# Two of the five 512-column blocks of w1 and w3 by seven block products in place of eight, in three feed-forward stages of a Trainium2 decoder trunk

## The chip, the cores and the metric

The kernel runs on one core of a Trainium2 chip. The metric is device time in microseconds of one execution, taken as the median over runs of the same program. A core has five engines with a queue of their own each: TensorE (PE; PEld is its weight load), VectorE (DVE), ScalarE (ACT), GpSimd (POOL) and SyncE (SP, which here issues nearly all DMAs). Each queue is worked off in order, and queues wait for each other through semaphores.

## The reference

The reference is a decoder trunk of two layers for 256 tokens of width 1024 in float32. What matters here is the feed-forward stage, which stands twice in each layer:

```
def _swiglu(x, w1, w3, w2):
    return (jax.nn.silu(x @ w1) * (x @ w3)) @ w2
...
    for l in range(DEPTH):
        h = _swiglu(x, ffn_w1[l, 0], ffn_w3[l, 0], ffn_w2[l, 0])
        x = _layernorm(ALPHA * x + 0.5 * h, ln_g[l, 0], ln_b[l, 0])
        h = _mixer(x, l, ...)
        x = _layernorm(ALPHA * x + h, ln_g[l, 1], ln_b[l, 1])
        h = _swiglu(x, ffn_w1[l, 1], ffn_w3[l, 1], ffn_w2[l, 1])
        x = _layernorm(ALPHA * x + 0.5 * h, ln_g[l, 2], ln_b[l, 2])
```

w1 and w3 are 1024 x 2816, w2 is 2816 x 1024. So there are four feed-forward stages and two mixer stages.

## The kernel before

**Numbers in two parts.** Every matrix product is made of three TensorE passes. A float32 value v is split into a rounded part hi and a rest lo = v - hi: ScalarE writes hi (an ACTIVATE Copy to float32r), VectorE writes lo (a TENSOR_TENSOR subtract). `three` then issues hi·x_hi, lo·x_hi and hi·x_lo into one PSUM bank. In a matmul of this kernel the stationary operand is a 128x128 tile of x (128 channels by 128 tokens), and the moving operand is 128 channels by 512 columns of the weight.

**Weights.** `stream` issues one DMA on SP for 128 x 2048 floats (1 MB) into one of four `raw` buffers (`RAW, HL = 4, 8`), and splits it in two pieces of 1024 elements per partition. A piece holds two channel tiles of 512 columns, and takes one of eight `hi` and one of eight `lo` buffers. In the blocks of w1 and w3 the split is made in operations of 512 elements (`sub=512`), elsewhere of 1024. A buffer of `hi` or `lo` comes free when the last matmul that reads it is done, a `raw` buffer when its last split is done.

**A feed-forward stage (`ffn`).** 20 of the 22 column tiles of w1 and w3 are made in five blocks (n = 0 to 4) of 512 columns by `gemm_b2`, the other two by `gemm_a2`; then `gemm_b` multiplies with w2. One block makes a 2 x 2 array of PSUM banks: t = 0, 1 for the two groups of 128 tokens, m = 0, 1 for w1 and w3. Its four MB of weights are loaded in the order (c, m), where c = 0, 1 is the lower and the upper half of the 1024 channels. The pass t = 0 takes them as they come, and the pass t = 1 takes the same pieces again:

```
for t in range(NT):
    order = second if t else (0, 1)
    for c in order:
        for m in range(2):
            if t == 0:
                got[m][2 * c : 2 * c + 2] = stream(srcs[m][:, c * CH : (c + 1) * CH], sub=512, ...)
            for i in range(2 * c, 2 * c + 2):
                rows_b(ps[t][m], t, 2 * i, got[m][i], xh, xl, KT, first=order[0] * KT // 2)
    done(t, ps[t])
```

One `rows_b` is six matmuls, a block 96. After each pass `done` of `front` runs a SiLU on ScalarE out of bank m = 0 (L612 before) and a product with bank m = 1 on VectorE (L613 before). Then `turned` moves the result into the other layout: two copies on GpSimd (`parted`, L193), a transposing DMA on SP (L197), two copies on GpSimd (`joined`, L202), and a split by ScalarE (hhi, L629) and VectorE (hlo, L631). Those results are read only by the product with w2.

**What sets the order.** TensorE's queue is the order of the program text (`manual_schedule`). For the other engines a scheduler places each instruction into its queue, by priorities that rise with every weight chunk (`step`) and by its own model of times; `issue_after` ties a few instructions behind others. Generators that are started with `beside` are continued by `beat`, which counts TensorE's work in units of 1024 moving columns times six matmuls; so the texts `yield 4` and `wait` are distances in TensorE's work.

**The norm ahead of a stage (`Norm`).** The layer norm of the stage before is finished while the next stage begins; `affine` writes the normalised rows in token-last layout (kept in float32 for a while in the tiles `xf` and `nvia`) and splits them into the new x tiles. `front` is 0 for the norm ahead of a mixer and not 0 for the norms ahead of three of the four feed-forward stages; the first stage has none. `tokens` then does four operations of 1024 elements on VectorE (L541 before).

Of the kernel before, what the change touches and what calls it, by code (L numbers as in the profile page):

```python
# [12 lines left out]
F32R = mybir.dt.float32r  # L13
# [4 lines left out]
ALU = mybir.AluOpType  # L18
AX = mybir.AxisListType

P = 128
# [33 lines left out]
def trunk(ctx, tc, x, xT, w13a, w13b, w2, wb, wqk, wu, wg, wgr, wbr, wbrr, wo, gateb, gatebr, sgug, sgub, sguwT, sgubias, lam, diffg,  # L55
# [18 lines left out]
    def name(s):  # L74
        serial[0] += 1
        return f"{s}_{serial[0]}"
# [4 lines left out]
    def side_bank():  # L81
        return psum.tile([P, 512], F32, tag="side", name=name("sbank"))
# [66 lines left out]

        return tc.issue_after(ins) if ins is not None else nullcontext()  # L150

    def stream(src, width=CH, sub=HC, lent=(), after=(None, None), pool=()):

        step()
        raw = raw_pool.tile([P, CH], F32, tag="raw", name=name("raw"))
        for g in gate:
            g[0] -= 1
        while len(gate) > 1 and gate[1][0] < 0:  # L160
            gate.pop(0)
        with behind(gate[0][1] if gate and gate[0][0] < 0 else None):
            loaded[0] = nc.sync.dma_start(raw[:, :width], src).ins
        out = []
        first = sooner.pop() if sooner else latest
        for o in range(0, width, HC):
            eng = G if o // HC in pool else V
            if o // HC in lent:
                hi, lo = ([act.tile([P, 512], F32R, tag="slot", name=name(n)) for _ in range(2)] for n in ("lhi", "llo"))
                at = [(hi[j], lo[j]) for j in range(2)]  # L170
            else:
                hi = hi_pool.tile([P, HC], F32R, tag="hi", name=name("whi"))
                lo = lo_pool.tile([P, HC], F32R, tag="lo", name=name("wlo"))
                at = [(hi[:, p : p + sub], lo[:, p : p + sub]) for p in range(0, HC, sub)]
            for p, (h, w) in zip(range(0, HC, sub), at):
                r = raw[:, o + p : o + p + sub]
                with behind(first[0]):
                    A.activation(h, r, AF.Copy)  # L178
                with behind(after[o // HC] or (first[1] if eng is V else None)):
                    eng.tensor_tensor(out=w, in0=r, in1=h.bitcast(F32), op=ALU.subtract)  # L180
            out.append((hi, lo))
        return out
# [134 lines left out]
    def gemm_b2(srcs, xh, xl, done, norm=None, second=(0, 1), each=None):  # L317
# [9 lines left out]
        for t in range(NT):  # L327
# [14 lines left out]
            with behind(latest[0] if t == 0 else None):  # L342
                done(t, ps[t])

    def gemm_first(srcs, done):

        step()
        ps = [[bank() for _ in range(2)] for _ in range(NT)]
        raw = [[raw_pool.tile([P, CH], F32, tag="raw", name=name("raw")) for _ in range(2)] for _ in range(2)]
        for k0, nk in ((0, 1), (1, 1), (2, 1), (3, 1), (4, 2), (6, 2)):  # L350
            xr = slots("xraw", 2)[0][:, : nk * T]
            nc.sync.dma_start(xr, xT[:, k0 * T : (k0 + nk) * T])
            c, k = k0 // 4, k0 % 4
            if nk == 2 or k % 2 == 0:
                w = [[p.tile([P, HC], F32R, tag=n, name=name("w" + n)) for p, n in ((hi_pool, "hi"), (lo_pool, "lo"))]
                     for _ in range(2)]
            for m in range(2):
                (A if k0 + m == 0 else nc.sync).dma_start(raw[c][m][:, k * 512 : (k + nk) * 512],
                                                          srcs[m][:, k0 * 512 : (k0 + nk) * 512])
            x = x_cat[c][:, k : k + nk]  # L360
            split(x[:, :, :T], x[:, :, T:], xr.rearrange("p (k t) -> p k t", k=nk))
            ws = [[[v[:, (k + j) % 2 * 512 : (k + j) % 2 * 512 + 512] for v in w[m]] for m in range(2)]
                  for j in range(nk)]
            for j in range(nk):
                for m in range(2):
                    split(*ws[j][m], raw[c][m][:, (k + j) * 512 : (k + j + 1) * 512])
            end = k0 + nk == KT
            for ts in ((0,), (1,)) if end else ((0, 1),):
                for j in range(nk):
# [67 lines left out]
    class Norm:  # L437
# [5 lines left out]

        def __init__(self, l, i, scale, eps, after, last=False):
            self.scale, self.eps, self.last, self.done, self.front = scale, eps, last, set(), i
            self.ends, self.xhi, self.xlo = [None] * NT, {}, {}
# [97 lines left out]
        def sent(self):  # L544
# [15 lines left out]
            self.affine(1, 0, self.via[1], self.via[1], (1, 1, 2), two[1])  # L560
            yield 1.7
            self.affine(1, 1, self.via[2], self.via[2], (2, 2), two[2])

        def affine(self, t, h, src, xf, pieces, two=None):
            self.done.add((t, h))
            k = 0
            with soon():
                for n in pieces:
# [30 lines left out]
    def ffn(l, f, i, norm, last=False):  # L599
# [445 lines left out]
```

## Time and profile before

| | |
|---|---|
| runs | median 1209.9 us, 1209.68 to 1210.15 (3 runs) |
| profiled execution | span 1208.3 us from its first to its last instruction; the page gives no device time of this execution beside it |
| PE busy | 1202.6 us, 5891 matmul records |
| DVE busy | 903.2 us (75%) |
| ACT busy | 719.9 us (60%) |
| POOL busy | 332.9 us (28%) |
| granted TensorE clock | 1.000 over the span |
| DMA | 263.58 MB, mean 218 GB/s |

A matmul's record is longer than the distance to the next, since matmuls are pipelined. So PE's busy time tells only that something was in the array; its pace is read from the distance of the block ends. In the first of the three stages that the change touches, layer 0's second feed-forward stage, the blocks lie as follows (by the SiLU operations at their ends): n = 1 from 441.9 us, n = 2 from 463.7, n = 3 from 485.5, n = 4 from 507.2 to 529.0.

### The profile page before, as it was taken

Reading aid. Unit: us, or ns where it says so; the run is one execution under the profiler, and the core shown is the slowest. Engines: PE = TensorE matmul, PEld = TensorE weight load, DVE = VectorE, ACT = ScalarE, POOL = GpSimd, SP = SyncE. Lnnn points to the kernel's source line nnn. Section 1 sums busy time; section 2 is a strip of 40 time slices with the busy share of each in tenths; the row PEclk is TensorE's granted clock in tenths of the full one; section 3 lists DMA queues with packets and bytes.
Section 4 is the critical chain, followed back from the end, with each engine's and each line's share of the span. In section 5 each row is a group of like instructions: output and inputs, shape, how many; then the busy total and the mean of one; then the engine's idle time right before and its main releaser. Section 6 shows DMA issues by size and latency. Waiting matters only on the chain.

```text
span 1208.3 us, 16816 instructions
## 1 busy us (share of the span) xinstructions
PE 1202.6 (100%) x5891; PEld 1013.3 (84%) x5891; DVE 903.2 (75%) x1544; ACT 719.9 (60%) x1388; POOL 332.9 (28%) x442
## 2 busy tenths in 40 slices
PE   9999999999999999999999999999999999999998
PEld 8888888888888888888888888888888888888887
DVE  6686669897689886766686756688966989776763
ACT  6465547668855665554555554576788556564740
POOL 1433101256421234330053330004464012423300
PEclk9999999999999999999999999999999999999999
DMA  9967646768765666767476766476676764877540
GB/s 347 303 219 238 253 174 203 259 200 231 240 213 180 200 231 208 249 201 261 149 245 198 259 187 261 148 273 238 211 205 199 251 192 153 274 231 239 186 181 35
DMA packets 124006, 263.58 MB, mean 218 GB/s; under 512 B 88417, under 2 KB 89489, under 8 KB 97809
## 3 DMA queue, kind: packets, MB, share of 16 engines
q1 hardware_dynamic: 119664, 248.80, 62.0%
q0 software_dynamic: 3824, 13.18, 3.4%
q8 instruction: 46, 0.75, 0.3%
q10 hardware_dynamic: 432, 0.52, 0.1%
q14 instruction: 40, 0.32, 0.1%
HBM read 236.52 MB, written 1.05 MB: 197 GB/s over the span
## 4 chain that ended last, share of the span: by engine, by line
PE 99%; DMA 0%; DVE 0%; ACT 0%; issue 0%; ACTq 0%
PE bank L256 72%; PE bank L268 15%; PE bank L275 8%; PE bank L374 2%; PE sbank L704 1%; PE sbank L760 1%; PE sbank L878 1%; DMA xraw<-in_xT 0%; PE sbank L758 0%; PE sbank L533 0%; PE sbank L512 0%; DVE xtok L520 0%; ACT whi L220 0%; DVE st L471 0%; DVE xtok L467 0%; ACT x L220 0%
## 5 line engine op out<-in xcount | busy, mean ns | idle before, releaser
L180 DVE TENSOR_TENSOR wlo<-raw,whi 128x512 fp32r<-128x512 f32 (+1 forms) x566 | 524.6, 962 | 114.8 <-ACT whi L178 80.0
L178 ACT ACTIVATE whi<-raw 128x512 fp32r<-128x512 f32 (+1 forms) x570 | 433.3, 799 | 246.6 <-PE bank L256 183.0
L256 PE MATMUL bank<-whi,x 128*128 128x512 f32 x1480 | 460.7, 390 | 0.0
L256 PEld LDWEIGHTS bank<-whi,x 128*128 128x128 f32 x1480 | 277.9, 188 | 57.7
L256 PE MATMUL bank<-wlo,x 128*128 128x512 f32 x740 | 288.0, 389 | 0.0
L256 PEld LDWEIGHTS bank<-wlo,x 128*128 128x128 f32 x740 | 139.0, 188 | 28.2
L268 PE MATMUL bank<-x,whi 128*128 128x512 f32 x640 | 153.3, 391 | 0.0
L256 PE MATMUL bank<-whi,hhi 128*128 128x512 f32 (+1 forms) x374 | 141.2, 378 | 0.0
L256 PE MATMUL bank<-wlo,hhi 128*128 128x512 f32 (+1 forms) x374 | 141.0, 377 | 0.0
L256 PE MATMUL bank<-whi,hlo 128*128 128x512 f32 (+1 forms) x374 | 140.9, 377 | 0.0
L193 POOL COPY planes<-planes 128x512 uint16<-128x512 uint16 x80 | 87.1, 1116 | 193.9 <-DVE planes L613 193.9
L268 PEld LDWEIGHTS bank<-x,whi 128*128 128x128 f32 x640 | 118.2, 188 | 23.8
L202 POOL COPY planes<-planes 128x512 uint16<-128x512 uint16 x80 | 70.9, 931 | 95.8 <-DMA planes<-planes 95.5
L613 DVE TENSOR_TENSOR planes<-planes,bank 128x512 f32<-128x512 f32 x40 | 27.4, 684 | 83.8 <-issue 69.3
L612 ACT ACTIVATE planes<-bank 128x512 f32<-128x512 f32 x40 | 23.9, 598 | 102.6 <-PE bank L256 101.5
L275 PEld LDWEIGHTS bank<-x,wlo 128*128 128x128 f32 x640 | 81.4, 191 | 2.9
L275 PE MATMUL bank<-x,wlo 128*128 128x256 f32 x640 | 82.6, 283 | 0.0
L256 PEld LDWEIGHTS bank<-whi,hlo 128*128 128x128 f32 x374 | 70.4, 188 | 13.0
L256 PEld LDWEIGHTS bank<-whi,hhi 128*128 128x128 f32 x374 | 70.4, 188 | 12.8
L256 PEld LDWEIGHTS bank<-wlo,hhi 128*128 128x128 f32 x374 | 70.4, 188 | 12.6
L575 POOL COPY nvia<-ntwo 128x256 uint16<-128x256 uint16 x20 | 10.4, 565 | 198.1 <-DMA ntwo<-nvia 179.9
L680 POOL TENSOR_TENSOR swap<-swap,sin_t 128x512 f32<-128x512 f32 x16 | 27.1, 1695 | 100.0 <-DMA swap<-z 78.0
(209 smaller groups left out, 1392.0 us busy)
## 6 DMA issues: line engine op xcount, KB each, us to landing
raw<-in_w13b SPq DMA_DIRECT2D x76, 1024.0 KB, 5.8
raw<-in_w SPq DMA_DIRECT2D x40, 1024.0 KB, 6.2
raw<-in_wb SPq DMA_DIRECT2D x16, 1024.0 KB, 5.1
raw<-in_wqk SPq DMA_DIRECT2D x16, 1024.0 KB, 6.3
raw<-in_w13a SPq DMA_DIRECT2D x8, 1024.0 KB, 5.1
raw<-in_wgr SPq DMA_DIRECT2D x8, 1024.0 KB, 5.3
raw<-in_wg SPq DMA_DIRECT2D x8, 1024.0 KB, 5.0
raw<-in_wu SPq DMA_DIRECT2D x8, 1024.0 KB, 6.4
```

The source lines that it names most:

```text
L178: A.activation(h, r, AF.Copy)
L180: eng.tensor_tensor(out=w, in0=r, in1=h.bitcast(F32), op=ALU.subtract)
L193: G.tensor_copy(out=planes(out)[:, w], in_=numbers(src)[:, w])
L202: eng.tensor_copy(out=numbers(out)[:, w], in_=planes(src)[:, w])
L256: PE.matmul(ps, xx, w, start=start and n == 0, stop=stop and n == 2)
L268: PE.matmul(b[-1], hi[:, k * P : (k + 1) * P], xc(k), start=k == 0, stop=False)
L275: PE.matmul(b[n][:, :T], lo[:, k * P : (k + 1) * P], xc(k)[:, :T], start=False, stop=k == KT - 1)
L374: PE.matmul(ps[t][m], x[:, j, o + t * P : o + (t + 1) * P], y, start=k0 + j == 0 and o == 0 and y is hi, stop=k0 + j == KT - 1 and y is lo)
L612: silu[0] = A.activation(s, ps[0], AF.Silu).ins
L613: added[0] = V.tensor_tensor(out=s, in0=s, in1=ps[1], op=ALU.mult).ins
L680: turned_by[0] = G.tensor_tensor(out=s3, in0=s3, in1=s, op=ALU.mult).ins
L704: PE.matmul(banks[m][:, j * nk : (j + 1) * nk], rows(qT, m, j, t * P, P), rows(kT, m, j, 0, nk), start=True, stop=True)
```

## The change

In the stages whose norm has `front` not 0 (layer 0 second, layer 1 first and second feed-forward stage), the blocks n = 2 and n = 4 are made by a new function, `gemm_seven`. It takes the 2 x 2 block form (x in token groups by channel halves, the weight in channel halves by w1, w3) and makes seven products of four channel tiles each, with 12 matmuls each, in place of eight. The sums on the weight side are made for each block by `differ` on VectorE, in place in the raw buffers. The sums on the x side are made once per stage by `Norm.seven`. Three side banks of PSUM are used; results are copied out by `kept` (ScalarE) and added on VectorE. The waits of the transposing steps of block n = 1 are one unit shorter in these stages.

```diff
+    def differ(out, a, b):
+        for o in range(0, CH, HC):
+            V.tensor_tensor(out=out[:, o : o + HC], in0=a[:, o : o + HC], in1=b[:, o : o + HC], op=ALU.subtract)
+
+    def gemm_seven(srcs, sums, done):
+        x11, x12, x22 = ((lambda k, o, h=h, t=t: x_cat[h][:, k, o + t * P : o + (t + 1) * P])
+                         for t, h in ((0, 0), (0, 1), (1, 1)))
+        s1, s2, s3, s4 = (lambda k, o, v=v: v[bool(o)][:, k * P : (k + 1) * P] for v in sums)
+        bx, by, bz = (side_bank() for _ in range(3))
+
+        def product(ps, x, w, first):
+            for k in range(KT // 2):
+                hi, lo = (v[:, k % 2 * 512 : k % 2 * 512 + 512] for v in w[k // 2])
+                for n, (y, o) in enumerate(((hi, 0), (lo, 0), (hi, T))):
+                    PE.matmul(ps, x(k, o), y, start=first and k == n == 0, stop=k == KT // 2 - 1 and n == 2,
+                              skip_group_check=True)
+                beat(0.25)
+
+        def kept(ps):
+            v = s512("part")
+            A.activation(v, ps, AF.Copy)
+            return v
+
+        (w11, w21), (w12, w22) = ((s[:, :CH], s[:, CH:]) for s in srcs)
+        w11 = fetch(w11)
+        product(bx, x11, pieces(w11), True)
+        w12 = fetch(w12)
+        differ(w11, w12, w11)
+        product(bz, s1, pieces(w11), True)
+        a, z = kept(bx), kept(bz)
+        w22 = fetch(w22)
+        differ(w11, w22, w11)
+        product(bx, s2, pieces(w11), False)
+        b = kept(bx)
+        product(bz, s4, pieces(w22), False)
+        w21 = fetch(w21)
+        differ(w12, w22, w12)
+        product(bx, s3, pieces(w12), False)
+        c = kept(bx)
+        product(by, x12, pieces(w21), True)
+        differ(w11, w21, w11)
+        V.tensor_tensor(out=a, in0=by, in1=a, op=ALU.add)
+        V.tensor_tensor(out=b, in0=bz, in1=b, op=ALU.add)
+        done(0, (a, b))
+        V.tensor_tensor(out=c, in0=c, in1=z, op=ALU.add)
+        product(bx, x22, pieces(w11), False)
+        done(1, (bx, c))
...
+            if self.front:
+                yield 4
+                yield from self.seven()
...
+        def seven(self):
+            x11, x12, x21, x22 = (self.rows[v] for v in ((0, 0), (0, 1), (1, 0), (1, 1)))
+            self.sums = [slots("sum", 4, F32R) for _ in range(4)]
+            for v, (out, a, b, op) in zip((0, 2, 1, 3), ((x22, x21, x22, ALU.add), (x21, x11, x21, ALU.subtract),
+                                                         (x11, x22, x11, ALU.subtract), (x12, x12, x11, ALU.subtract))):
+                V.tensor_tensor(out=out, in0=a, in1=b, op=op)
+                split(*self.sums[v], out)
+                yield 1
...
+            elif n in (2, 4) and norm:
+                gemm_seven(srcs, norm.sums, front(n, (10.3, 10.3)))
             else:
-                gemm_b2(srcs, xh, xl, front(n, (13.3, 10.3)), norm=norm if n == 0 else None)
+                early = norm is not None and n == 1
+                gemm_b2(srcs, xh, xl, front(n, (13.3 - early, 10.3 - early)), norm=norm if n == 0 else None)
```

`fetch` is the loading part of `stream`, taken out of it. `pieces` splits one raw buffer into two hi and two lo buffers with operations of 1024 elements. In the changed file these lines have other numbers: `split` is L225 (ScalarE) and L227 (VectorE), `differ` L363, the matmul of `product` L381, `kept` L387, the three additions L408, L409 and L411, the SiLU L696, the product behind it L697, hlo L715.

In the built program of the changed kernel VectorE's queue has, at the end of such a block (block n = 2 of the stage above; out<-in, rows that follow each other):

```
L227 TensorTensor wlo<-raw,whi 128x1024           (w21, first half)
L227 TensorTensor wlo<-raw,whi 128x1024           (w21, second half)
L363 TensorTensor raw<-raw,raw 128x1024 x2        (difference for the seventh product)
L408 TensorTensor part<-sbank,part 128x512        (a = by + a; waits for the sixth product's last matmul)
L409 TensorTensor part<-sbank,part 128x512        (b = bz + b)
L411 TensorTensor part<-part,part 128x512         (c = c + z)
L697 TensorTensor planes<-planes,part 128x512     (SiLU(a) times b)
L227 TensorTensor wlo<-raw,whi 128x1024           (seventh product, first half)
L227 TensorTensor wlo<-raw,whi 128x1024           (seventh product, second half)
```

More of the change, by code (lines that the diff above doesn't have):

```diff
@@ L150, in behind, with fetch @@
         return tc.issue_after(ins) if ins is not None else nullcontext()
-    def stream(src, width=CH, sub=HC, lent=(), after=(None, None), pool=()):
+    def fetch(src, width=CH):
         step()
@@ L163, in stream @@
             loaded[0] = nc.sync.dma_start(raw[:, :width], src).ins
+        return raw
+    def stream(src, width=CH, sub=HC, lent=(), after=(None, None), pool=()):
+        raw = fetch(src, width)
         out = []
@@ L343, in gemm_b2, with pieces @@
                 done(t, ps[t])
+    def pieces(raw):
+        out = []
+        for o in range(0, CH, HC):
+            hi = hi_pool.tile([P, HC], F32R, tag="hi", name=name("whi"))
+            lo = lo_pool.tile([P, HC], F32R, tag="lo", name=name("wlo"))
+            split(hi, lo, raw[:, o : o + HC])
+            out.append((hi, lo))
+        return out
+    def differ(out, a, b):
+        for o in range(0, CH, HC):
+            V.tensor_tensor(out=out[:, o : o + HC], in0=a[:, o : o + HC], in1=b[:, o : o + HC], op=ALU.subtract)
[39 more added lines that the diff above has]
+        done(1, (bx, c))
     def gemm_first(srcs, done):
@@ L445, in __init__ @@
             self.scale, self.eps, self.last, self.done, self.front = scale, eps, last, set(), i
-            self.ends, self.xhi, self.xlo = [None] * NT, {}, {}
+            self.ends, self.xhi, self.xlo, self.rows = [None] * NT, {}, {}, {}
             self.gT, self.bT = (v[:, l, i] for v in (ln_g, ln_b))
@@ L562, in sent @@
             self.affine(1, 1, self.via[2], self.via[2], (2, 2), two[2])
+            if self.front:
+                yield 4
+                yield from self.seven()
         def affine(self, t, h, src, xf, pieces, two=None):
             self.done.add((t, h))
+            self.rows[t, h] = xf
             k = 0
```

## Prediction

> **What bounds the kernel now.** I read the page first: the busy times, the slices and the chain of work that ended last.
>
> ```profile
> span 1208.3 us, 16816 instructions
> PE 1202.6 (100%) x5891; PEld 1013.3 (84%) x5891; DVE 903.2 (75%) x1544; ACT 719.9 (60%) x1388; POOL 332.9 (28%) x442
> PE 99%; DMA 0%; DVE 0%; ACT 0%; issue 0%; ACTq 0%
> ```
>
> TensorE is the bound: 99% of the chain, with nothing to name between its matmuls. What a matmul is worth is read from the distance of block ends, in ScalarE's timeline (start, duration, what was waited for):
>
> ```profile
> 452.82 0.60 ACT L612 ACTIVATE planes<-bank 128x512 f32<-128x512 f32 x1 [7.01 <-PE bank L256]
> 463.70 0.60 ACT L612 ACTIVATE planes<-bank 128x512 f32<-128x512 f32 x1 [0.16 <-PE bank L256]
> 474.58 0.60 ACT L612 ACTIVATE planes<-bank 128x512 f32<-128x512 f32 x1 [6.55 <-PE bank L256]
> L256 PE MATMUL bank<-whi,x 128*128 128x512 f32 x1480 | 460.7, 390 | 0.0
> ```
>
> Each pass of 48 matmuls takes 10.88 us, a block 21.76, a matmul 10.88 / 48 = 0.2267 us; its record is 0.390 long, so its end lies 0.16 after the next could start. Then I asked for the four blocks n = 1 to 4 of this stage (columns: length, then busy time and count by engine):
>
> ```profile
> 441.90:463.70 21.80, 21.80 (x98) 18.05 (x97) 17.69 (x26) 10.24 (x19) 11.07 (x8) 1.00 0.65 196
> 463.70:485.50 21.80, 21.80 (x98) 18.03 (x97) 14.69 (x25) 11.35 (x23) 6.59 (x8) 1.00 0.68 239
> 485.50:507.20 21.70, 21.70 (x97) 18.00 (x96) 15.07 (x23) 11.27 (x22) 6.75 (x8) 1.00 0.66 217
> 507.20:529.00 21.80, 21.80 (x97) 18.03 (x97) 14.40 (x19) 10.88 (x18) 6.72 (x8) 1.00 0.70 203
> ```
>
> VectorE (third pair) has 7 us to spare in a block of 21.8, and only 4 in n = 1, where the norm is still being finished. That slack is what the change spends.
>
> **Part 1, what is removed.** Each of six blocks (two in each of three stages) issues 7 x 12 = 84 matmuls of the same shape in place of 96. 12 x 0.2267 = 2.72 us a block, 16.3 us in all, at full value, since nothing else is on the chain. A block would take 19.04 us.
>
> **Part 2, what VectorE gets.** Prices, from its timeline (the first two rows give pitches by their starts):
>
> ```profile
> 448.01 1.21 DVE L541 TENSOR_TENSOR xtok<-xtok,bc 128x1024 f32<-128x1024 f32 x1
> 449.15 0.68 DVE L180 TENSOR_TENSOR wlo<-raw,whi 128x512 fp32r<-128x512 f32 x1
> 449.75 1.21 DVE L541 TENSOR_TENSOR xtok<-xtok,bc 128x1024 f32<-128x1024 f32 x1
> 450.89 1.88 DVE L180 TENSOR_TENSOR wlo<-raw,whi 128x512 fp32r<-128x512 f32 x3
> 469.90 0.74 DVE L631 TENSOR_TENSOR hlo<-planes,hhi 128x256 fp32r<-128x256 f32 x2
> 530.87 1.23 DVE L180 TENSOR_TENSOR wlo<-raw,whi 128x1024 fp32r<-128x1024 f32 x1 [0.92 <-ACT whi L178]
> ```
>
> So 1024 wide: pitch 1.14, duration 1.23. 512 wide: 0.60 and 0.68. hlo: 0.37. A block had 16 lo subtractions of 512 (9.6 us), two products behind the SiLU (1.2) and four hlo (1.5), 12.3 bare. It gets 14 lo subtractions and 8 differences of 1024 (25.1), three additions (1.8), and the same products and hlo: 29.6 bare, against 19.04 of TensorE. Some of it can be done ahead. How much, the built order says: behind the seven wide operations that serve the first two products stands the SiLU product of the block ahead, which waits for that block's last matmul. Everything later is made while TensorE works.
>
> I walk that queue for one block, time 0 being the start of the first product. The SiLU can start at 0.16 and takes 0.60; VectorE's product is issued at 0.8, the next operation at 1.4. Up to the additions follow two differences and two lo for the third product, two lo for the fourth, two for the fifth (its differences were made ahead), two for the sixth, two differences for the seventh, and four hlo: 12 x 1.14 + 4 x 0.37 = 15.2. Since each difference must land before ScalarE can round it, a little is lost: I allow 0.8. VectorE reaches the additions at 17.4. TensorE ends its sixth product at 6 x 2.72 + 0.16 = 16.5. So without any disturbance VectorE is just behind.
>
> GpSimd disturbs it:
>
> ```profile
> 499.87 1.49 POOL L193 COPY planes<-planes 128x512 uint16<-128x512 uint16 x2 [3.72 <-DVE planes L613]
> 489.02 2.72 DVE L180 TENSOR_TENSOR wlo<-raw,whi 128x512 fp32r<-128x512 f32 x3
> 489.24 1.96 POOL L193 COPY planes<-planes 128x512 uint16<-128x512 uint16 x2 [9.63 <-DVE planes L613]
> 532.01 0.68 DVE L613 TENSOR_TENSOR planes<-planes,bank 128x512 f32<-128x512 f32 x1
> 532.61 3.27 DVE L180 TENSOR_TENSOR wlo<-raw,whi 128x1024 fp32r<-128x1024 f32 x2
> ```
>
> A pair of copies takes 1.49, 0.75 each. Three lo that take 1.88 alone take 2.72 beside a pair; two wide ones take 3.27 for 1.14 + 1.23 = 2.37. A pair thus costs VectorE 0.84 to 0.90, if it meets a full queue. Up to three of a block's four pairs fall ahead of the additions: 0 to 2.5 us. [...]
>
> **Part 3, the wait that is added.** The three additions and the first SiLU product stand ahead of the seventh product's two lo subtractions, and the first addition waits for the sixth product's last matmul. Behind it queue exactly the operands of the next 12 matmuls. From the moment when VectorE is free and that matmul has ended: 3 x 0.60 + 0.60 + 1.23 = 3.63 until the first lo lands. TensorE can run one matmul (hi) meanwhile. Were VectorE early, the stall would be 0.16 + 3.63 - 0.2267, with semaphores some 3.7 us: more than the 2.72 saved. ScalarE's SiLU of a (0.60) runs beside the second and third addition. With VectorE at the additions at 17.4 the lo lands at 21.0 where TensorE wanted it at 16.6: a loss of 4.5. The parting copies of the first SiLU product start with these two lo, as in the last row above: 0.45 on the first, 0.45 on the second, of which the second is mostly covered by the half product (1.36). So 5.0 undisturbed before. With one and a half pairs of copies ahead of the additions I take 1.6 more: **6.6 us a block** (bounds 3.7, VectorE early, and 7.5, all pairs meet it).
>
> **Part 4, the rest.** Norm.seven adds four sums and four splits of 512 a stage, 8 x 0.60 = 4.8 on VectorE in block n = 1, where 4.1 were free and the work ahead now has four wide differences more (4.6). Part of it shifts into the lead: I take 1 us a stage (bounds 0 and 3). ScalarE: 14 roundings of 1024, three copies and two SiLU of 512 (0.60 each) and four hhi a block, from
>
> ```profile
> L178 ACT ACTIVATE whi<-raw 128x1024 fp32r<-128x1024 f32 x5 | 5.3, 1064 | 4.1 <-PE bank L256 4.1
> L629 ACT ACTIVATE hhi<-planes 128x256 fp32r<-128x256 f32 x12 | 4.6, 407 | 0.0
> raw<-in_w13b SPq DMA_DIRECT2D x76, 1024.0 KB, 5.8
> ```
>
> 14.9 + 3.0 + 1.6 = 19.5, less than VectorE's share and inside the longer block: nothing. A copy out of PSUM must end before the bank is written again; one product (2.72) lies between and covers 0.6; without it 0.6 each. Loads: their number and sizes stay, but the raw buffers are held longer. The last one, w11, is free when the seventh lo is made, about 23; 5.8 later it holds the last quarter of the next block, wanted three quarters of a pass later, at 25 + 8.2 = 33: hidden with 4 us to spare; any lateness beyond that would be paid one for one. What the copies and transposes give is read by w2's product alone, behind the whole stage: nothing.
>
> **Part 5, the clock.** TensorE was idle for long only at the very end (its last timeline row, and two windows behind it, where the third number from the end is the granted clock):
>
> ```profile
> 1202.97 1.56 PE L512 MATMUL sbank<-bc,minus 128*128 128x256 f32 x4 [0.66 <-ACT minus L510]
> 1204.50:1207.30 2.80, 0.02 (x1) 0.00 (x0) 0.75 (x1) 0.00 (x0) 0.00 (x0) 1.00 0.51 187
> 1207.40:1208.30 0.90, 0.00 (x0) 0.00 (x0) 0.00 (x0) 0.00 (x0) 0.00 (x0) 0.50 0.00 0
> ```
>
> The last matmul ended at 1204.5, and 2.8 us later the clock was halved. The new stalls leave TensorE idle for 3.7 us and more, so I expect this inside the kernel. How long it lasts no row shows; if as long as the idle time that brought it, 2.8 us at half pace lose 1.4. I take 1.5 for four of the six: 6 us (bounds 0 and 6 x 3). [...]
>
> **Sum**, against the profiled execution's span: 1208.3 - 16.3 + 6 x 6.6 + 3 x 1 + 6 = 1240.6. The median of the runs lies 1.6 above that span, so 1242.
>
> **Rivals.** *Stalls without the clock* (28%): as above with a clock at 1.00; 1242 - 6 = 1236. For: the drop was seen once only, and the idle stretches are broken by one matmul. *VectorE is early* (10%): copies miss its full stretches and its lead is larger; only the floor is lost, 1209.9 - 16.3 + 6 x 3.7 = 1216. Against: 29.6 bare us a block. *Heavy* (10%): all pairs meet it, n = 1 pays 3, every stall costs 3 us of clock: 1209.9 - 16.3 + 45 + 9 + 18 = 1266. *Faster* (4%): the seventh product's lo are not late, because the stage behind the addition is shorter than rows say. It decides at 2.72: if wait, additions and lo took TensorE less than that, the change would win; were it 1.5, 1209.9 - 16.3 + 9 = 1203. For: VectorE's other halves, such as operations of 256, are short. Against: each of the five operations has its row, and none may overtake in a queue that is worked off in order. *No change* (3%) needs the same chain at 2.3 to 3.1. That the change removes fewer matmuls than it says can be left out: the built program has 5671 in place of 5743, 72 less.
>
> **How the numbers follow.** Forecast with the clock 45%, without it 28, early 10, heavy 10, faster 4, same 3. The range must leave out at most 2 in 10: it cuts the faster and same cases, half of the early and most of the heavy one: 1217 to 1262. Slower by over 0.2% (2.4 us, about what a measurement of this kernel tells from no change): 93%.
>
> **What would show it.** In the profile after: six gaps on PE of 3.7 us or more, each in L381 behind its first matmul on the seventh product, ended by VectorE's lo (L227), behind L408 to L411 and L697; blocks n = 2 and n = 4 of 25 to 27 us, n = 3 near 22; DVE near full in them; PEclk below 1.00 in slices of the three stages. I am wrong if these blocks take under 21.8, if PE waits there for DMA, or if the gaps sit at the first products, which would put it down to VectorE's lead and not to the order.

## The result and the profile after

| | before | after |
|---|---|---|
| median | 1209.9 us | 1257.9 us (1257.13 to 1259.01, 4 runs) |
| ratio | | 1.0398, 95% interval 1.0383 to 1.0413 |
| profiled execution, span | 1208.3 us | 1255.4 us |
| mean granted TensorE clock | 1.000 | 0.985 |

The changed kernel is 48 us slower: the forecast of 1242 had the direction right and was 16 us short, inside its range. The page of the changed kernel first (the span; busy times by engine; the granted clock in 40 slices):

```profile
span 1255.4 us, 16779 instructions
PE 1212.1 (97%) x5819; PEld 1009.8 (80%) x5819; DVE 1032.8 (82%) x1622; ACT 767.1 (61%) x1412; POOL 390.8 (31%) x442
PEclk9999999999999999989999999999999999979999
```

VectorE is busy for 130 us more, and TensorE is no longer busy throughout. The view of waits on TensorE names what it waits for (engine, tile and line; us in total, times, longest one):

```profile
PE sbank L381 <- DVE wlo L227: 29.2, 12, 4.0
PE bank L261 <- DVE silu L283: 2.6, 3, 1.1
```

The kernel before has no such wait in these stages. Twelve waits for VectorE's lo are two for each of the six blocks: the forecast had one each. The windows of the six blocks, from their first matmul to the next block's (start:end, length, busy time and count of PE, PEld, DVE, ACT, POOL, then granted clock, DMA share, GB/s):

```profile
467.09:495.64 28.55, 21.56 (x86) 16.66 (x84) 28.55 (x30) 20.15 (x30) 9.70 (x8) 0.94 0.48 141
517.78:545.11 27.33, 22.43 (x86) 17.28 (x85) 27.33 (x29) 18.85 (x25) 8.98 (x6) 0.89 0.54 162
662.59:689.48 26.89, 21.77 (x85) 16.75 (x84) 26.89 (x28) 18.94 (x29) 9.17 (x8) 0.94 0.53 152
711.92:740.59 28.67, 23.11 (x85) 17.91 (x84) 27.35 (x28) 18.94 (x25) 9.46 (x7) 0.88 0.51 142
1094.06:1125.75 31.69, 25.03 (x85) 19.38 (x84) 29.07 (x31) 20.18 (x30) 10.44 (x8) 0.79 0.48 139
1147.70:1174.70 27.00, 22.32 (x86) 16.45 (x84) 27.00 (x28) 18.47 (x25) 11.71 (x7) 0.94 0.51 148
```

The blocks take 26.9 to 31.7 us in place of 21.8 before, and VectorE is busy for all of it in four of them. At 0.2267 us for each matmul a block would take 19.04. What the starts of the matmuls show beyond that is about 6.7 us of stall a block (40.1 in all: 2.1 at the third product and 4.5 at the seventh, the remainder at a few single matmuls) and about 15.5 us in all of matmuls at half clock. VectorE's timeline shows the first of these blocks (start, duration, form; rows without a bracket followed at once on the one before):

```profile
467.16 1.21 DVE L227 TENSOR_TENSOR wlo<-raw,whi 128x1024 fp32r<-128x1024 f32 x1
468.29 1.21 DVE L363 TENSOR_TENSOR raw<-raw,raw 128x1024 f32<-128x1024 f32 x1
469.43 1.21 DVE L227 TENSOR_TENSOR wlo<-raw,whi 128x1024 fp32r<-128x1024 f32 x1
470.56 0.67 DVE L697 TENSOR_TENSOR planes<-planes,bank 128x512 f32<-128x512 f32 x1
471.16 2.76 DVE L363 TENSOR_TENSOR raw<-raw,raw 128x1024 f32<-128x1024 f32 x2
...
484.68 2.35 DVE L363 TENSOR_TENSOR raw<-raw,raw 128x1024 f32<-128x1024 f32 x2
486.95 0.68 DVE L408 TENSOR_TENSOR part<-sbank,part 128x512 f32<-128x512 f32 x1
487.56 0.68 DVE L409 TENSOR_TENSOR part<-sbank,part 128x512 f32<-128x512 f32 x1
488.15 0.68 DVE L411 TENSOR_TENSOR part<-part,part 128x512 f32<-128x512 f32 x1
488.75 1.18 DVE L697 TENSOR_TENSOR planes<-planes,part 128x512 f32<-128x512 f32 x1
489.86 3.27 DVE L227 TENSOR_TENSOR wlo<-raw,whi 128x1024 fp32r<-128x1024 f32 x2
```

The SiLU product of the block ahead (L697 at 470.56) stands 3.47 us behind the block's start, where the prediction had 0.8: VectorE was not waiting for it but still at the second product's operands. ScalarE's SiLU had long been done:

```profile
464.57 0.60 ACT L696 ACTIVATE planes<-bank 128x512 f32<-128x512 f32 x1 [0.91 <-PE bank L261]
```

It reads only the bank of w1, which is complete 12 matmuls before the block ends at 467.09. So the block ends that were read from the SiLU operations of the kernel before lie some 2.5 us early (by TensorE's timeline its n = 2 starts at 466.22 and not at 463.70); their distances, and with them the price of a matmul, are not touched by that.

Since VectorE is behind, the differences for the third product come late, TensorE waits there, and again at the seventh, where the additions stand before the lo:

```profile
474.06 0.50 PE L381 MATMUL sbank<-whi,sum 128*128 128x512 f32 x1 [1.37 <-ACT part L387]
475.86 0.50 PE L381 MATMUL sbank<-wlo,sum 128*128 128x512 f32 x1 [1.30 <-DVE wlo L227]
...
487.10 0.50 PE L381 MATMUL sbank<-whi,x 128*128 128x512 f32 x1 [0.29 <-ACT whi L225]
491.63 0.79 PE L381 MATMUL sbank<-wlo,x 128*128 128x512 f32 x1 [4.03 <-DVE wlo L227]
```

### The profile page after: what moved, and what is told of

It is laid out like the page before. It is cut to its first block, busy times and chain, and to the rows that moved or that the text cites. A ratio compares the mean times of both kernels' runs of the same rounds, so it can differ in the third digit from the quotient of the medians.

```text
span 1255.4 us, 16779 instructions
## 1 busy us (share of the span) xinstructions
PE 1212.1 (97%) x5819; PEld 1009.8 (80%) x5819; DVE 1032.8 (82%) x1622; ACT 767.1 (61%) x1412; POOL 390.8 (31%) x442
## 5 line engine op out<-in xcount | busy, mean ns | idle before, releaser
L185 DVE TENSOR_TENSOR wlo<-raw,whi 128x1024 fp32r<-128x1024 f32 (+1 forms) x470 | 462.9, 1021 | 82.4 <-ACT whi L183 62.5
L183 ACT ACTIVATE whi<-raw 128x512 fp32r<-128x512 f32 (+1 forms) x474 | 375.8, 833 | 191.9 <-PE bank L261 126.8
L261 PE MATMUL bank<-whi,x 128*128 128x512 f32 x1096 | 343.2, 390 | 0.0
L261 PEld LDWEIGHTS bank<-whi,x 128*128 128x128 f32 x1096 | 206.0, 188 | 42.2
L261 PE MATMUL bank<-wlo,x 128*128 128x512 f32 x548 | 214.1, 391 | 1.2 <-DVE wlo L185 1.1
L198 POOL COPY planes<-planes 128x512 uint16<-128x512 uint16 x80 | 122.9, 1563 | 132.0 <-DVE planes L697 132.0
L207 POOL COPY planes<-planes 128x512 uint16<-128x512 uint16 x80 | 92.5, 1201 | 155.4 <-DMA planes<-planes 155.4
L225 ACT ACTIVATE whi<-raw 128x1024 fp32r<-128x1024 f32 (+1 forms) x100 | 97.1, 988 | 54.4 <-DVE raw L363 46.6
L227 DVE TENSOR_TENSOR wlo<-raw,whi 128x1024 fp32r<-128x1024 f32 (+1 forms) x100 | 120.5, 1232 | 4.8 <-ACT whi L225 4.6
L261 PEld LDWEIGHTS bank<-wlo,x 128*128 128x128 f32 x548 | 103.0, 188 | 25.4 <-DVE wlo L185 4.4
L381 PE MATMUL sbank<-whi,sum 128*128 128x512 f32 x192 | 65.2, 412 | 3.3 <-ACT part L387 3.2
```

The source lines that it names most:

```text
L198: G.tensor_copy(out=planes(out)[:, w], in_=numbers(src)[:, w])
L207: eng.tensor_copy(out=numbers(out)[:, w], in_=planes(src)[:, w])
L225: a = A.activation(hi, src, AF.Copy).ins
L227: return a, eng.tensor_tensor(out=lo, in0=src, in1=hi.bitcast(F32), op=ALU.subtract).ins
L261: PE.matmul(ps, xx, w, start=start and n == 0, stop=stop and n == 2)
L381: PE.matmul(ps, x(k, o), y, start=first and k == n == 0, stop=k == KT // 2 - 1 and n == 2, skip_group_check=True)
```

## The experiments

The theories at the start: **A, the order** (the additions and the SiLU product ahead of the seventh product's lo); **B, the amount** of VectorE's work, whatever its order; and **C, the half clock**. In the short diffs, lines are shortened to what changes.

**1. The order alone.** The seventh product's lo are issued ahead of the additions and the SiLU product.

```diff
+        seventh = pieces(w11)
+        with behind(halved[0]):        # halved: the last lo of those pieces
             V.tensor_tensor(out=a, in0=by, in1=a, op=ALU.add)
...
-        product(bx, x22, pieces(w11), False)
+        product(bx, x22, seventh, False)
```

> The seventh product's two lo subtractions are put ahead of the three additions and the first SiLU product in VectorE's queue (the additions are issued behind the second lo). Nothing else changes. Theory A (order: the stall of 3.5 to 4.5 us on the seventh product is made by the additions' wait for the sixth product): the lo land 3.3 us earlier, the idle stretches fall under 1.5 us, the granted clock goes back to about 1.00, and the time falls by 6 x 3.3 + 14 = 34 us, to about 1224. Theory B (amount: VectorE is simply full, and the order decides only where TensorE waits): what is saved on the seventh product is paid in the next block; 1245 to 1255, with new gaps in blocks n = 3.

Measured: 1241.75 us (1240.78 to 1242.83), ratio to before 1.0264, 1.0247 to 1.0281. The order is worth 16.2 us, 2.7 a block, and 32 us of loss stay. The distance of the first two matmuls of the seventh product, 3.5 to 4.5 us in the changed kernel, falls to 1.3 at most; the stall at the third product stays; and a new wait stands at the start of n = 3 (waits on TensorE):

```profile
PE sbank L383 <- DVE wlo L227: 11.6, 12, 1.4
PE bank L261 <- DVE wlo L185: 8.3, 6, 2.5
```

It lies between the two forecasts, 1224 by A and 1245 to 1255 by B, and has the new gaps in n = 3 that B expected: both are at work.

**2. The amount alone.** `differ` does nothing, so the products are made with the plain weights. The scheduler then places the seventh product's lo ahead of the additions by itself.

```diff
     def differ(out, a, b):
-        for o in range(0, CH, HC):
-            V.tensor_tensor(out=out[:, o : o + HC], ..., op=ALU.subtract)
+        pass
```

> The weight differences are left out (the products take the raw weights, so the output differs): 8 operations of 1024 elements less per block on VectorE. In the built order the scheduler then also puts the seventh product's lo ahead of the additions. Both theories: with amount and order relieved nothing is left to wait for; the 72 matmuls come out in full, 1209.9 - 16.3 = 1194, up to 1198 with the sums of the norm. Above 1200 would mean a third cost (banks, loads).

Measured: 1213.72 us, ratio 1.0032, 1.0019 to 1.0045. All six blocks take exactly 19.04 us, without a stall. But the time is 16 to 20 us above what was expected, so there is a third cost. The waits on TensorE and TensorE's own timeline put it at the start of w2, after block n = 4; ScalarE's and SP's queues show why:

```profile
PE bank L261 <- DVE silu L283: 11.0, 3, 3.7
```
```profile
541.33 0.79 PE L261 MATMUL bank<-whi,hhi 128*128 128x512 f32 x1 [3.68 <-DVE silu L283]
```
```profile
539.49 1.06 ACT L183 ACTIVATE whi<-raw 128x1024 fp32r<-128x1024 f32 x1 [6.50 <-DMA raw<-in_w]
540.45 0.37 ACT L281 ACTIVATE r<-bank 128x256 f32<-128x256 f32 x1
```
```profile
532.64 1.23 SPq L202 DMA_TRANSPOSE planes<-planes  x1
533.97 0.53 SPq L161 DMA_DIRECT2D raw<-in_w  x1
```

VectorE's product of the last two column tiles (L283) waits for L281, which stands on ScalarE behind a rounding that waits for a piece of w2 for 6.5 us; that piece's load is issued at 533.97, behind a transposing DMA of block n = 4. In the kernel before the two outputs of a block come 11 us apart; by seven both come at its end, and so do their transposes.

**3. That third cost.** As experiment 2, with the transposing DMAs of n = 4 one unit of TensorE's work later, behind w2's first four loads on SP.

```diff
-                gemm_seven(srcs, norm.sums, front(n, (10.3, 10.3)))
+                gemm_seven(srcs, norm.sums, front(n, (11.3, 11.3) if n == 4 else (10.3, 10.3)))
```

> As e2_no_differ (no differences on the weight side, the seventh product's lo ahead of the additions), and for n = 4 the transposing DMAs of a pass are issued later (11.3 in place of 10.3), so that on SP all four loads of w2's first pieces stand ahead of them. Theory: e2's rest against the bare 16.3 us of gain, 20 us, lies at the start of w2, where the fourth load stands behind a transposing DMA and ScalarE's queue behind that load; three waits of 3.9 and the half clock of 5.3 behind them go, at most 17 us: 1197 to 1203. Rival: the wait is for the last block's own chain (SiLU, copies, transposes all at the block's end), whichever queue it stands in: 1212 to 1215.

Measured: 1196.78 us (1196.18 to 1197.5), ratio 0.9893, 0.9880 to 0.9907. The theory holds. SP now has

```profile
521.50 5.35 SPq L161 DMA_DIRECT2D raw<-in_w  x4
533.29 1.23 SPq L202 DMA_TRANSPOSE planes<-planes  x1
```

and no wait at w2 is left. This also prices the half clock where TensorE is the bound: experiment 2 had waits of 11.0 us and lost about 5.3 us in matmuls at half clock behind them, 16.3 together, and its profiled span is 16.5 us longer (1211.0 against 1194.5). And nearly the whole saving of the 72 matmuls comes out: in full it would give 1209.9 - 16.3 = 1193.6, and 3.2 of it are lost elsewhere.

**4. The same edit with the differences back**, the whole computation: experiment 1 with the later transposes.

> The whole computation: as e1_lo_first, with the same later transposing DMAs for n = 4. Theory: the wait of 1.5 us at the start of w2 goes in three stages, 1241.75 - 4.5 = 1237. Rival: VectorE's amount of work is the bound in these stages and the wait only moves: 1241 to 1242.

Measured: 1241.14 us, ratio 1.0258, 1.0244 to 1.0272. Nothing is gained against experiment 1. The rival has the right number, but the wait didn't move: it stayed at the start of w2, 3.9 us in three waits against 4.1 before the edit, though the four loads now stand ahead of the transposes on SP. With the differences VectorE itself is late there; its product L283 follows six lo subtractions without a pause:

```profile
544.35 8.55 DVE L185 TENSOR_TENSOR wlo<-raw,whi 128x1024 fp32r<-128x1024 f32 x6
552.82 0.41 DVE L283 TENSOR_TENSOR silu<-bank,r 128x256 f32<-128x256 f32 x1
```

Against experiment 3 the only difference in the work is `differ`: 48 operations of 1.14 us, 54.7 us on VectorE, cost 44.4 us of time. (The additions are tied behind the lo here; in experiment 3 the scheduler put them later by itself, among the lo of the next block. Experiment 12 tries a later place with the differences and gains nothing.)

**5. The order without the differences.** As experiment 2, with the additions and the SiLU product held ahead of the seventh product's lo as in the changed kernel.

```diff
-            split(hi, lo, raw[:, o : o + HC])
+            split(hi, lo, raw[:, o : o + HC], after=(None, hold))
...
-        product(bx, x22, pieces(w11), False)
+        product(bx, x22, pieces(w11, added[0]), False)   # added: the SiLU product
```

> As the kernel without differences, but the seventh product's lo are issued behind the first SiLU product, so that the order of the changed kernel is restored while VectorE has 9 us less per block. Theory A: the floor of the stall stays, one addition, the SiLU, the product and one lo after the sixth product, about 3.3 us a block: 1194 + 6 x 3.3 = 1214, and some us of lowered clock, 1214 to 1225. Theory B: VectorE has time to spare, the order costs next to nothing: 1194 to 1200.

Measured: 1244.81 us, ratio 1.0291, 1.0275 to 1.0306. Against experiment 2 the order costs 31.1 us, 5.2 a block, and not the 3.3 of the additions and lo alone, because VectorE's queue also waits for ScalarE's SiLU, which the scheduler put behind the next block's roundings, and these wait for a load (ScalarE, then VectorE):

```profile
483.44 2.19 ACT L183 ACTIVATE whi<-raw 128x512 fp32r<-128x512 f32 x4 [0.83 <-DMA raw<-in_w13b]
485.53 0.61 ACT L695 ACTIVATE planes<-part 128x512 f32<-128x512 f32 x1
```
```profile
486.17 0.69 DVE L696 TENSOR_TENSOR planes<-planes,part 128x512 f32<-128x512 f32 x1 [2.47 <-ACT planes L695]
```

With experiments 1 and 2 and the changed kernel this is a two by two table:

| | additions first | lo first |
|---|---|---|
| with differences | 1257.9 | 1241.75 |
| without | 1244.8 | 1213.7 |

The last cell holds some 17 us of w2's start, which experiment 3 takes away and which experiment 5 doesn't have (no wait for L283 in its list). With experiment 3's 1196.8 in that cell the order costs 48 us without the differences and 16 with them, and the differences cost 13 us with the additions first and 45 with the lo first. So the costs of order and amount can't be added: they hide each other, since both make VectorE late for the same matmuls.

**6. The clock alone.** The changed kernel with 14 matmuls more, into a spare bank, behind the first matmul of the seventh product, so that the array isn't idle there.

```diff
+                    for _ in range(fill if k == n == 0 else 0):
+                        PE.matmul(spare, x(0, 0), x_cat[0][:, 0], start=True, stop=True, ...)
...
-        product(bx, x22, pieces(w11), False)
+        product(bx, x22, pieces(w11), False, fill=14)
```

> Behind the first matmul of each seventh product TensorE runs 14 matmuls into a bank that nobody reads (3.2 us, less than each of the stalls of 3.5 to 4.5 us there). The work and all waits stay. If the lowered clock of the changed kernel (39 us of the span at 0.50) comes from these idle stretches and costs what the slower matmuls add up to (16 us): the clock stays at 1.00 and the time falls to about 1243. If the clock in the records costs nothing, or follows something else: 1257 to 1260.

Measured: 1261.48 us (1258.81 to 1263.63), ratio 1.0423, 1.0407 to 1.044. Within the span the time at half clock falls from 37.5 to 20.5 us (from 11 pieces of 3.41 us to 6), matmuls lose about 9 us to it in place of about 16, and nothing comes back. The time went to the next places that need VectorE: the three blocks n = 3 take 3.9 us more than in the changed kernel, and the waits on TensorE show the start of w2 (2.6 us there in the changed kernel):

```profile
PE sbank L381 <- DVE wlo L227: 12.1, 11, 1.4
PE bank L261 <- DVE silu L283: 8.0, 3, 2.9
```

So theory C gets no support in this kernel: where VectorE is late, half of the half clock could go without any gain in time. The other half stayed, so this is shown for half of it only. (The 14 matmuls, 3.3 us, fit into the gap and delay nothing by themselves except where it was shorter.)

**7. The fixed cost.** All blocks by `gemm_b2` as before, with the sums on the x side kept.

```diff
-            elif n in (2, 4) and norm:
+            elif False:
```

> All five blocks of a stage by gemm_b2 as before; the four sums and their splits on the x side (Norm.seven) stay, and so do the shorter waits of n = 1. It measures the change's fixed cost by itself. The prediction's Part 4 has 1 us a stage (0 to 3): 1213, at most 1219. The trace after shows n = 0 and n = 1 together 0.5 to 1.3 us longer in each stage, 2.5 in all: 1212.5. Rival: the lengthening of n = 1 is VectorE's lead for the first block by seven (the work ahead for n = 2) and not the sums; then 1210 to 1211.

Measured: 1212.09 us against 1209.64, ratio 1.0020, 1.0011 to 1.0029: 2.45 us, 0.8 a stage.

**8. A difference on GpSimd.** As experiment 4, with the fifth product's difference (w22 - w12) by GpSimd.

```diff
-        differ(w12, w22, w12)
+        differ(w12, w22, w12, G)
```

> As e7_lo_first_late, with one of the four differences of each block (w12 - w22, the operand of the fifth product) made by GpSimd in place of VectorE. VectorE is given 2.28 us less a block. If GpSimd needs 0.75 per 512 elements as in its copies, it works 3 us a block longer and holds VectorE up by 0.43 for each 0.75, 1.7 us: a net gain of 0.6 a block, 3.4 us below e7. Rival: it is slower than that, the fifth product waits for it and VectorE is held up for longer than the difference took: 3 us or more above e7.

Measured: 1258.2 us, ratio 1.0399, 1.0383 to 1.0415: 17 us slower than experiment 4. One pair of operations after another, from the timelines of VectorE and GpSimd, and the longest entry of the waits on TensorE:

```profile
466.34 3.37 POOL L365 TENSOR_TENSOR raw<-raw,raw 128x1024 f32<-128x1024 f32 x1
467.37 3.43 DVE L365 TENSOR_TENSOR raw<-raw,raw 128x1024 f32<-128x1024 f32 x1
469.67 3.36 POOL L365 TENSOR_TENSOR raw<-raw,raw 128x1024 f32<-128x1024 f32 x1
470.73 3.39 DVE L227 TENSOR_TENSOR wlo<-raw,whi 128x1024 fp32r<-128x1024 f32 x1
```
```profile
PE sbank L383 <- DVE wlo L227: 22.6, 12, 2.4
```

Beside VectorE, GpSimd's subtraction takes 3.36 us, and VectorE's operation beside it takes as long, in place of 1.2. In the whole kernel VectorE is busy for 1040.9 us, against 1030.2 in experiment 4, with 12 operations less. The rival is right that VectorE is held up for longer than the difference took. But the fifth product never waits for GpSimd's result: by the starts of the matmuls the stalls lie in the second and third product of each block, whose lo VectorE makes at that time.

**9. Half of the differences.** As experiment 4 without the first two differences of each block.

> As e7_lo_first_late, without the first two of the four differences of each block (the operands of the second and the third product are then the plain weights, the output is another). VectorE is given 4.56 us less a block, 25.0 bare in place of 29.6; without any difference it was 20.5. Theory L, VectorE's amount is paid in proportion: half of the 44.4 us between e7 (1241.1) and e6 (1196.8): 1219. Rival T, a threshold: a block by seven and the plain block before or behind it give VectorE 19.0 + 21.8 = 40.8 us of TensorE's work for 25.0 + 14.7 = 39.7 us of its own, so it just keeps up, the stalls at the third product go with its two differences, and what is left is paid little: 1205 or less. Rival S, the stalls belong to the seventh product's own two differences and to the order there: 1230 or more.

Measured: 1224.07 us (1220.73 to 1225.61), ratio 1.0114, 1.0097 to 1.0131; undecided, since another wait came in. No third product waits any more, but the first matmul of every seventh product waits for the copy of the fifth product's bank, which ScalarE had behind next-block roundings and a rounding that waits for VectorE (waits on TensorE, then ScalarE):

```profile
PE sbank L383 <- ACT part L389: 12.9, 6, 3.4
```
```profile
1088.90 1.06 ACT L225 ACTIVATE whi<-raw 128x1024 fp32r<-128x1024 f32 x1 [6.73 <-DVE raw L365]
1089.86 2.69 ACT L183 ACTIVATE whi<-raw 128x512 fp32r<-128x512 f32 x5
1092.46 0.58 ACT L389 ACTIVATE part<-sbank 128x512 f32<-128x512 f32 x1
```

**10. The same with that copy first.**

```diff
-        seventh = pieces(w11)
+        seventh = pieces(w11, copied[0])     # the roundings behind the copy
```

> As e9_half_differ (half of the differences left out), with the copy of the fifth product's bank (c) ahead of the seventh product's roundings in ScalarE's queue. In e9 the first matmul of the seventh product waited 1.0 to 3.6 us in all six blocks for that copy, which stood behind roundings that waited for VectorE's last difference and behind next-block roundings, and no block waited at its third product any more. Theory T (threshold: at 25.0 us of VectorE work a block keeps up): these waits of 13.8 us in all and the half clock of 5 behind them go, 1224.1 - 19 = 1205, at most 1210. Theory L (in proportion to the differences): what is taken from these waits comes back as waits for VectorE's lo, 1217 to 1222.

Measured: 1216.51 us (1215.56 to 1218.32), ratio 1.0056, 1.0041 to 1.0071. Five of the six blocks take 19.3 to 19.6 us, the full saving, and yet it is at the lower end of theory L, not at T: the debt is paid at the start of the plain block n = 3 and of w2.

```profile
PE bank L261 <- DVE wlo L185: 8.1, 7, 2.3
PE bank L261 <- DVE silu L283: 2.7, 3, 1.3
```

None, half and all of the differences thus give 1196.8, 1216.5 and 1241.1: 19.7 us for the first 27.4 us of VectorE's work and 24.6 for the second, 0.72 and 0.90 for one. This is rough, since of the three only this run has the copy put first.

**11. One block by seven.** As experiment 4, with only n = 2 by seven.

```diff
-            elif n in (2, 4) and norm:
+            elif n == 2 and norm:
```

> The whole computation: as e7_lo_first_late, with block n = 2 by seven and n = 4 by gemm_b2 as in the kernel before. The sums on the x side (2.5 us, measured alone) stay. Theory L, each block pays for itself: half of 1241.1 - 1209.6 - 2.5 = 29, so 1209.6 + 2.5 + 14.5 = 1226.6. Rival T: what the block leaves undone on VectorE is made good in the two plain blocks behind it, each with 7 us to spare, so that nothing is lost at n = 3 and at the start of w2: 3 us a stage less than by L, 1217. Rival S: VectorE's lead cannot be longer than the four raw buffers let it be, so the two blocks never hurt each other: as by L.

Measured: 1231.98 us, ratio 1.0186, 1.0169 to 1.0203: 5 us above theories L and S and 15 above T, so all three missed. A stage loses 7.4 us by n = 2 and only 3.1 more by n = 4: behind a block by seven n = 3 takes 26.2 us in place of 21.8 (2.4 of it at its first lo, the rest at the next ones), and n = 4, ahead of w2, pays less there. The plain block behind doesn't absorb the debt, since its first operands are what is late.

**12. The additions later still.** As experiment 4, with the additions and SiLU products of n = 2 behind the first four lo of n = 3.

```diff
+        if late is None:
+            finish()                    # additions and SiLU products
+        else:
+            late.append(lambda: (finish(), done(1, (bx, c))))   # called in n = 3, after its first piece
```

> The whole computation: as e7_lo_first_late, with the additions and the SiLU products of block n = 2 behind the first four lo subtractions of block n = 3. In e7 n = 3's first lo waits behind them, 2.4 us on TensorE in each of three stages. Theory: those 7.2 us go, since n = 3 gives VectorE 7 us to catch up: 1234, a little less with the half clock. Rival: VectorE is behind by a fixed amount of work at the end of n = 2, whichever order it is done in, and the wait moves into n = 3 or to the third product of n = 4: 1239 to 1241.

Measured: 1246.02 us, ratio 1.0300, 1.0282 to 1.0317: worse than experiment 4 by 5 us, so both theories missed. The wait moved to the fifth lo of n = 3 and grew there (the waits for L185 are 11.4 us, against 7.9):

```profile
489.45 3.53 DVE L185 TENSOR_TENSOR wlo<-raw,whi 128x512 fp32r<-128x512 f32 x4
492.91 0.68 DVE L416 TENSOR_TENSOR part<-sbank,part 128x512 f32<-128x512 f32 x1
```

Together with experiment 4 this suggests a debt of VectorE's that a change of order moves rather than pays; but it isn't of a fixed size, since other changes of order were worth 16 us (experiment 1) and 8 (experiment 10). No version with the whole computation beat the kernel before. The bound on what could be had is experiment 3, 13 us under it, with the differences at no cost. That the weights be loaded as sums, so that VectorE has fewer differences, was not tried.

## Why the prediction was right or wrong

From the bare saving (1193.6) the runs give one path to the changed kernel: 3.2 us of fixed cost and small waits (experiment 3, of which experiment 7 shows 2.45 as the sums), 44.4 for the differences (experiment 4), 16.8 for the order (the changed kernel against experiment 4): 1258.0. By the other path through the table the shares differ; only the sum is fixed.

**Part 1, right.** 84 matmuls at 0.2267 take 19.04 us; the blocks of experiments 2 and 3 take just that.

**Part 2 and 3: the size right, the place partly wrong.** Forecast 6.6 us of stall a block, measured 6.7, and VectorE is full as said. But 2.1 of it lie at the third product. The step that failed is the walk's beginning: the SiLU product at 0.8 was at 3.47, because the work ahead of it was not done in time. (The SiLU, put at 0.16, had in fact run before the block's start, which by itself would have made VectorE earlier.) Of GpSimd's copies one pair met VectorE ahead of the additions in the block shown, for some 0.8 us (the rows at 471.16 and 473.85); no run took the copies away, so their share isn't measured apart. The prediction said that gaps at earlier products would put the loss down to VectorE's lead and not to the order; a third of it is that, and experiment 1 shows the consequence: the order is worth 2.7 us a block, not the 3.7 and more of the floor.

**Part 4: the sums right, the nothings wrong.** One us a stage was forecast for the sums, 0.8 measured. "What the copies and transposes give is read by w2's product alone: nothing" failed: w2's start lost 17 us in experiment 2 through SP's and ScalarE's queues (from the end of n = 4, three stages). In the changed kernel it lost 3.5 up to w2's first matmul, and there the reason is VectorE, as in experiment 4: from 547.62 on it makes six lo in 9.26 us without a pause, and L283 stands behind them. ScalarE's copies out of PSUM were covered in the changed kernel, since the lo came later still (1.37 us, then 1.30 more); with VectorE relieved they cost 12.9 us of waits (experiment 9). n = 3, taken as unchanged, lost 1.25.

**Part 5, the mis-sized term in the trace's account.** Forecast 6 us, measured 15.5 in the blocks: 11 pieces of 3.41 us at half clock, 1.4 us each, not four events of 1.5; the price of one was right, the number was not, because the third product's stall brought some too and some lasted for two pieces. That four of the six stalls would bring it was an estimate, which no run shows: each of the six blocks has at least one piece, the one from 1094.06 four. Of the 15.7 us between sum and measurement this is 9.5, w2's start 3.5 and n = 3 1.25. As a cause it is weaker than as an entry: experiment 6 took nearly half of it away and no time came back. The forecast's entry and the rival without the clock are therefore both only half right.

**Rivals.** VectorE early is refuted by its full windows. Heavy had the right neighbours (copies, clock) but not n = 1, which experiment 7 shows to be cheap. Faster is refuted by the wait of 4.03 us against its limit of 2.72.

## What to carry to other kernels

When an algorithm trades TensorE's products for vector operations, sum VectorE's bare time over the block and the blocks beside it against TensorE's new time: here each us of added VectorE work cost 0.7 to 0.9 us although the engine's average was 75% busy before. Moving work in VectorE's full queue moved the wait (in experiment 1 from 3.5 to 4.5 us at the seventh product to as much as 2.5 at the start of n = 3); look where it lands (the next block's first operand, the next product) before counting it as gained. And when two results that used to be staggered come together, follow their transposes and copies through every queue they share with the next stage's loads (some 17 us at the start of w2 in experiment 2).

## What the runs showed of the hardware

**The clock fell after windows that were not idle.** The half-clock pieces of each run start on one grid of 3.41 us. I counted the matmul work in each window of that grid, 0.2267 us for a matmul of 512 columns and in proportion for fewer, over the windows at full clock in all fourteen traces. The 57 windows that were followed by half clock had at most 0.42 of their time in matmul work, and the other 4886 had at least 0.39; only a few lie between. (The last norm's matmuls of 512 columns are 0.43 us apart, as at 1250.61 and 1251.04 in the changed kernel; counted so, the window from 1248.96 there has 0.46, at 0.2267 it would have 0.22.) In the changed kernel the eight windows ahead of half clock had 0.00, 0.00, 0.12, 0.14, 0.26, 0.27, 0.28 and 0.39. One of the windows at half clock there, behind the stall at the seventh product:

```profile
491.21:494.62 3.41, 2.99 (x7) 2.41 (x8) 3.41 (x4) 2.77 (x6) 3.02 (x3) 0.50 0.84 214
```

So the clock fell after windows without any matmul work and also after windows that were up to two fifths busy: in six of the eight, the work of some two to six matmuls (0.12 to 0.39 of 3.41 us) did not keep it up. How a window that is itself at half clock is counted is not settled.

**Beside GpSimd's subtraction, VectorE's operation ended 1.09 us behind it.** In the rows of experiment 8 VectorE's operation starts at 467.37, GpSimd's beside it ends at 469.71, and VectorE's ends at 470.80, 1.09 us later. Alone such an operation takes a pitch of 1.14, so its whole work fits behind the end of GpSimd's. It is the same at 473.03 and 474.12, and beside all twelve of GpSimd's subtractions (1.08 to 1.09 us). Beside GpSimd's copies VectorE lost less than their recorded time, 0.84 to 0.90 for a pair of 1.49 in the rows of the prediction; why is not settled.
